# Three small unread tiles that shift the on-chip addresses of x's parts, the weights' parts and the small tiles

## The chip, the core and the metric

The kernel runs on one core of a Trainium2 chip, from one launch. The metric is the device time of that core in microseconds (us), as the median of repeated runs. All data lie in HBM at the start; the core has an on-chip memory of 128 partitions (SBUF), an accumulator memory (PSUM), and engines that run side by side: TensorE multiplies matrices, VectorE (DVE) and ScalarE (ACT) work element by element, GpSimd (POOL) does a little of both and issues some DMAs, and SyncE (SP) issues the others. A matmul on TensorE has two operands in SBUF: a stationary one of 128 x 128 elements, which is loaded first (a weight load, PEld in the profile), and a moving one of up to 512 columns, which is streamed through it.

## The reference, cut to what matters

The reference is a two-layer sequence encoder over 512 positions of 1024 channels in float32. Layer 0 mixes positions with a gated delta rule (8 heads, chunks of 64), layer 1 with gated linear attention (4 heads, chunks of 64). Each mixer is followed by a residual and a LayerNorm, then by a squared-ReLU MLP with 4096 hidden features, again with a residual and a LayerNorm.

```python
for i in range(DEPTH):                      # DEPTH = 2
    m = _mixer_gdn(x, ...) if i % 2 == 0 else _mixer_gla(x, ...)
    x = _layernorm(DEEPNORM_ALPHA * x + m, ln1_g[i], ln1_b[i])
    a = relu(matmul(x, mlp_w1[i]))          # 512 x 1024 by 1024 x 4096
    x = _layernorm(DEEPNORM_ALPHA * x + matmul(a * a, mlp_w2[i]), ln2_g[i], ln2_b[i])
```

Most of the arithmetic is in the large products: the input and output projections of the mixers and the two matrices of each MLP.

## The kernel before

**Products in three parts.** Every large float32 product is made of three matmuls. `split` (L85) turns a float32 tile into a high part (ACT, L96 or L106: the value rounded to the format fp32r) and a low part (DVE, L101: what the rounding left). `mm3` (L119 to L124) then issues high x high, high x low and low x high into the same PSUM bank. The weights are loaded by SP into `wst` tiles (L106, L115), and their parts go to `wh` and `wl`. The activations x stand transposed as `xth` and `xtl` (128 partitions, 8 blocks of 128 channels, 512 positions).

**Stages, in order.** `gdn` (to about 430 us): for each of 8 heads four projections of 128 columns (`pjk`, `pjq`, `pjv`, `pjz`: x moving, weights stationary, 512 columns), with the chunk work of other heads between them; then the output projection (`oa`, `ob`: weights moving). `mlp` of layer 0 (to about 740 us), `gla` (to about 990 us; `pjv` has x as the stationary operand and the weights moving), `mlp` of layer 1 (to the end).

**The MLP.** The first matrix of a group of features is multiplied with Strassen's scheme on 2 x 2 blocks (`Pair.products`, L475): seven products of 256 columns into the banks `fx` and `fyz`. Three of them read slices of `xth` and `xtl`; four read sums of such blocks, which `x_blocks` (L407) builds once per layer and splits into `xh3`, `xl3`, `xh5` ... `xl7` (printed by the profile as `xh` and `xl`). The stationary operand of all seven is a part of the weights in `wh` and `wl`. The second matrix (`second`, L548) goes the same way with 512 columns into `pX`, `pY`, `pZ`: the moving operand is `w2h` or `w2l`, the stationary one `ah` or `al`. In the main loop (L744) TensorE alternates: 12 matmuls of 256 columns (`fx`, `fyz`), then 6 of 512 columns (`pX`, `pY`, `pZ`), in an order written out by hand (`in_order`).

**Where tiles lie.** Each tile gets a fixed byte offset, the same in all 128 partitions, when the program is built. Pools stand one behind the other in the order in which `body` opens them (L1802): `const`, `big`, `wst`, `whl`, `small`, and behind these the pools of a stage. Inside a pool the tiles stand in the order of their first use; each is rounded up to 32 bytes. In the kernel before:

| tiles | pool | first offset | offset mod 128 |
|---|---|---|---|
| `ident`, five biases | const | 4224 | 0 (`ident`) |
| `xt0` to `xt3` (also `oh`), `xth`, `xtl` | big | 4896 | 32 |
| `wst` (3 buffers) | wst | 54048 | 32 |
| `wh`, `wl` (3 buffers each) | whl | 66336 | 32 |
| row statistics and the like | small | 90912 | 0 to 96 |
| constants for layer 1 (992 bytes, open from the first MLP to the end of `gla`) | gcst | 93984 | 32 |
| first MLP: `h`, `ah`, `al`, `w2r`, `w2h`, `w2l`, `xh`, `xl` | mlp | 94976 | 0 |
| second MLP: the same tiles, with no `gcst` ahead of them | mlp | 93984 | 32 |
| gla: `oth`, `otl`, `q`, `k`, `v` and others | gla | 94976 | 0 |
| gdn: `ol`, `sil`, `kt`, `qd` and others | gdn | 124800 | 0 |

All the large tiles are multiples of 128 bytes long, and the slices that the matmuls take (a block of 128 weight columns is 512 bytes, a block of 256 positions 1024 bytes) keep the offset of their tile mod 128.

Of the kernel before, what the change touches and what calls it, by code (L numbers as in the profile page):

```python
# [8 lines left out]
F32 = mybir.dt.float32  # L9
# [8 lines left out]
P = 128  # L18
# [10 lines left out]
class Ctx:  # L29


    def __init__(self, tc, nc, pools):
        self.tc, self.nc = tc, nc
        self.const, self.big, self.wst, self.whl, self.small = pools
        nc_ = nc
        self.ident = self.const.tile([P, P], F32, name="ident")
        make_identity(nc_, self.ident[:, :])

        self.bias = {}
        for i, v in enumerate((LN_EPS, RMS_EPS, -0.5 * math.log(P), 1.0 / D, -1.0 / D)):  # L40
            self.bias[v] = self.const.tile([P, 1], F32, name=f"bias{i}")
            nc.vector.memset(self.bias[v], v)
        self.xth = self.xtl = self.xt = None
        self.dma_i = 0
        nc.scalar.preload_act_table_set("natural_log_exp_and_others")

    def dma(self, out, in_):
# [1782 lines left out]
```

## Time and profile before

| | |
|---|---|
| median of 3 runs | 1331.79 us (1331.76 to 1331.99) |
| time of the profiled execution | 1330.95 us |
| its span, first to last instruction | 1329.0 us |
| mean granted TensorE clock | 0.997 |
| TensorE matmuls in the trace | 8659 |
| VectorE busy | 1108.9 us (83%) |
| ScalarE busy | 805.3 us (61%) |
| HBM read, written | 113.99 MB, 2.10 MB |

The profile comes from one execution. Its page gives busy times, 40 equal slices of the span, the chain of work that ended last, and groups of instructions by source line and tile. Matmuls overlap each other: the recorded length of one runs from its start to the (modelled) time its last result is out, so the sum of lengths says more than the engine can do, and what counts is the step from the start of one matmul to the start of the next. The timeline gives these starts. TensorE's line of the page covers the union of the recorded lengths.

### The profile page before, as it was taken

Reading aid. Unit: us, or ns where it says so; the run is one execution under the profiler, and the core shown is the slowest. Engines: PE = TensorE matmul, PEld = TensorE weight load, DVE = VectorE, ACT = ScalarE, POOL = GpSimd, SP = SyncE. Lnnn points to the kernel's source line nnn. Section 1 sums busy time; section 2 is a strip of 40 time slices with the busy share of each in tenths; the row PEclk is TensorE's granted clock in tenths of the full one; section 3 lists DMA queues with packets and bytes.
Section 4 is the critical chain, followed back from the end, with each engine's and each line's share of the span. In section 5 each row is a group of like instructions: output and inputs, shape, how many; then the busy total and the mean of one; then the engine's idle time right before and its main releaser. Section 6 shows DMA issues by size and latency. Waiting matters only on the chain.

```text
span 1329.0 us, 22303 instructions
## 1 busy us (share of the span) xinstructions
PE 1310.3 (99%) x8659; PEld 1120.2 (84%) x8659; DVE 1108.9 (83%) x1818; ACT 805.3 (61%) x1598; POOL 124.7 (9%) x177
## 2 busy tenths in 40 slices
PE   9999999999999999999999999999999999999996
PEld 7777877777877889999998888888889899999985
DVE  7787888878768988989988787867878789889888
ACT  4757666767643666566667754554466466566656
POOL 5000000000001810101101200000001001101011
PEclk9999999999999999999999999999999999999998
DMA  5210110111232574575548521211217365556465
GB/s 182 95 49 33 55 59 34 63 49 56 73 112 96 176 179 153 145 196 152 149 146 169 154 85 64 75 53 64 96 63 226 94 196 151 146 172 157 145 140 145
DMA packets 44044, 154.35 MB, mean 116 GB/s; under 512 B 5419, under 2 KB 5795, under 8 KB 43939
## 3 DMA queue, kind: packets, MB, share of 16 engines
q1 hardware_dynamic: 32163, 110.85, 24.6%
q0 software_dynamic: 11776, 42.08, 15.9%
q8 instruction: 68, 1.11, 0.3%
q14 instruction: 37, 0.30, 0.1%
HBM read 113.99 MB, written 2.10 MB: 87 GB/s over the span
## 4 chain that ended last, share of the span: by engine, by line
PE 92%; DVE 4%; ACT 3%; issue 1%; DVEq 0%; POOL 0%; ACTq 0%; POOLq 0%
PE fx L124 3%; PE fx L123 3%; PE fx L122 3%; PE pX L123 3%; PE pX L122 3%; PE pX L124 3%; PE pjv L122 3%; PE pjv L123 3%; PE pjv L124 3%; PE m L1692 3%; PE fyz L124 3%; PE fyz L122 3%; PE fyz L123 3%; PE pY L123 2%; PE pY L122 2%; PE pY L124 2%
## 5 line engine op out<-in xcount | busy, mean ns | idle before, releaser
L96 ACT CAST wh<-wst 128x1024 fp32r<-128x1024 f32 x152 | 159.5, 1049 | 115.9 <-PE fyz L123 38.2
L101 DVE TENSOR_TENSOR wl<-wst,wh 128x1024 fp32r<-128x1024 f32 x150 | 184.7, 1232 | 46.1 <-ACT wh L96 45.3
L101 DVE TENSOR_TENSOR w2l<-w2r,w2h 128x1024 fp32r<-128x1024 f32 x92 | 112.5, 1223 | 22.2 <-ACT w2h L96 22.2
L96 ACT CAST w2h<-w2r 128x1024 fp32r<-128x1024 f32 x94 | 98.4, 1048 | 45.1 <-PE pX L124 16.7
L400 POOL DMA_DIRECT2D w2r<-w2r x56 | 48.5, 896 | 497.4 <-DVE w2l L101 252.9
L96 ACT CAST ah<-h 128x1024 fp32r<-128x1024 f32 x56 | 58.9, 1051 | 40.4 <-PE pX L123 18.3
L448 DVE TENSOR_TENSOR wst<-wst 128x512 f32<-128x512 f32 x120 | 80.0, 688 | 0.4
L101 DVE TENSOR_TENSOR al<-h,ah 128x1024 fp32r<-128x1024 f32 x56 | 68.5, 1223 | 4.4 <-ACT ah L96 4.4
L123 PE MATMUL pX<-w2l,ah 128*128 128x512 f32 x168 | 66.2, 394 | 0.0
L122 PE MATMUL pX<-w2h,ah 128*128 128x512 f32 x168 | 66.1, 393 | 0.0
L124 PE MATMUL pX<-w2h,al 128*128 128x512 f32 x168 | 65.7, 391 | 0.0
L122 PE MATMUL pjv<-wh,xth 128*128 128x512 f32 x128 | 54.4, 425 | 0.0
L124 PE MATMUL fx<-xh,wl 128*128 128x256 f32 x192 | 54.3, 283 | 0.0
L124 PE MATMUL fyz<-xh,wl 128*128 128x256 f32 x192 | 54.2, 282 | 0.0
L122 PE MATMUL fx<-xth,wh 128*128 128x256 f32 x192 | 54.2, 282 | 0.0
L124 PE MATMUL fx<-xth,wl 128*128 128x256 f32 x192 | 54.2, 282 | 0.0
L123 PE MATMUL fx<-xtl,wh 128*128 128x256 f32 x192 | 54.2, 282 | 0.0
L122 PE MATMUL fyz<-xh,wh 128*128 128x256 f32 x192 | 54.2, 282 | 0.0
L123 PE MATMUL fx<-xl,wh 128*128 128x256 f32 x192 | 54.1, 282 | 0.0
L123 PE MATMUL fyz<-xl,wh 128*128 128x256 f32 x192 | 54.0, 281 | 0.0
L122 PE MATMUL fx<-xh,wh 128*128 128x256 f32 x192 | 53.8, 280 | 0.0
L123 PE MATMUL pj<-xtl,wh 128*128 128x256 f32 (+1 forms) x160 | 52.2, 328 | 0.2 <-DVE xtl L188 0.2
(536 smaller groups left out, 4326.2 us busy)
## 6 DMA issues: line engine op xcount, KB each, us to landing
wst<-in_w SPq DMA_DIRECT2D x68, 512.0 KB, 4.3
w2r<-in_w SPq DMA_DIRECT2D x60, 512.0 KB, 3.8
w2r<-w2r POOLq DMA_DIRECT2D x56, 512.0 KB, 5.3
wst<-in_a_in SPq DMA_DIRECT2D x32, 512.0 KB, 3.3
wst<-in_b_vr SPq DMA_DIRECT2D x16, 512.0 KB, 3.4
wst<-in_a_out SPq DMA_DIRECT2D x8, 512.0 KB, 3.3
wst<-in_b_in SPq DMA_DIRECT2D x8, 512.0 KB, 3.4
wst<-in_b_out SPq DMA_DIRECT2D x8, 512.0 KB, 3.3
```

Of the source, the lines that this page charges most:

```text
L96: h = nc.scalar.copy(hi, src)
L101: self.halves = h, nc.vector.tensor_tensor(lo, src, hi.bitcast(F32), ALU.subtract)
L122: mm(ps, ah, bh, start=start, stop=False, **kw)
L123: mm(ps, ah, bl, start=False, stop=False, **kw)
L124: self.last_mm = mm(ps, al, bh, start=False, stop=stop, **kw)
L400: nc.gpsimd.dma_start(blocks[a + (q,)], blocks[b + (q,)], accum_op=ALU.add)
L448: plus = lambda a, b: V.tensor_tensor(a, a, b, ALU.add)
L1692: T.matmul(ps[:, d, :], *ops(d), start=True, stop=True)
```

## The change

Three tiles are added that nothing reads: 96 bytes per partition at the end of `const`, 64 bytes at the head of `whl`, and 96 bytes at the head of `small`. Each is written once by a memset on VectorE.

```diff
         self.xth = self.xtl = self.xt = None
         self.dma_i = 0
+        for pool, n in ((self.const, 24), (self.whl, 16), (self.small, 24)):
+            nc.vector.memset(pool.tile([P, n], F32, name="room", bufs=1), 0.0)
         nc.scalar.preload_act_table_set("natural_log_exp_and_others")
```

The tiles behind them move. With the table above: `xt`, `xth`, `xtl` and `wst` move by 96 bytes, from 32 to 0 mod 128. `wh` and `wl` move by 160, from 32 to 64 mod 128. Everything behind `small`'s new tile moves by 256, so its offset mod 128 stays: the tiles of the first MLP, of `gla` and of `gdn` listed above stay at 0, those of the second MLP at 32. No instruction of the rest of the program is added, removed or reordered in the source.

## The prediction

> **What bounds the kernel now.** I read the page first, for the engine that sets the end.
>
> ```profile
> PE 1310.3 (99%) x8659; PEld 1120.2 (84%) x8659; DVE 1108.9 (83%) x1818; ACT 805.3 (61%) x1598; POOL 124.7 (9%) x177
> ...
> PE   9999999999999999999999999999999999999996
> ...
> PEclk9999999999999999999999999999999999999998
> ...
> PE 92%; DVE 4%; ACT 3%; issue 1%; DVEq 0%; POOL 0%; ACTq 0%; POOLq 0%
> ```
>
> TensorE is busy in every slice at full clock, and 92% of the chain that ended last is its own. DVE and ACT have slack. So a byte offset is worth what it does to the step from one matmul to the next. The timeline gives steps, and the layout table says which operands they join. Here are five runs of matmuls without a break, each by its first and a later start.
>
> ```profile
> 433.17 0.28 PE L122 MATMUL pj<-xth,wh 128*128 128x256 f32 x1
> ...
> 440.73 0.28 PE L122 MATMUL pj<-xth,wh 128*128 128x256 f32 x1
> ...
> 441.08 0.28 PE L122 MATMUL pj<-xth,ah 128*128 128x256 f32 x1
> ...
> 443.77 0.28 PE L124 MATMUL pj<-xth,al 128*128 128x256 f32 x1
> ...
> 500.95 0.28 PE L122 MATMUL fyz<-xh,wh 128*128 128x256 f32 x1
> ...
> 502.37 0.40 PE L122 MATMUL pX<-w2h,ah 128*128 128x512 f32 x1
> ...
> 704.64 0.40 PE L122 MATMUL pX<-wh,ah 128*128 128x512 f32 x1
> ...
> 707.44 0.40 PE L122 MATMUL pY<-w2h,ah 128*128 128x512 f32 x1
> ...
> 713.14 0.39 PE L123 MATMUL pZ<-w2l,ah 128*128 128x512 f32 x1
> ...
> 717.90 0.39 PE L123 MATMUL pZ<-xl,ah 128*128 128x512 f32 x1
> ```
>
> 256 columns, both operands at 32 mod 128: 63 steps in 7.56 us, 120 ns each. Moving at 32, stationary at 0: 23 steps in 2.69 us, 117 ns. Moving at 0, stationary at 32: 12 steps in 1.42 us, 118.3 ns. 512 columns, moving at 32, stationary at 0: 12 steps in 2.80 us, 233.3 ns. Both at 0: 21 steps in 4.76 us, 226.7 ns. So the offset of one operand against the other is seen: 32 bytes apart, short matmuls gain 2 to 3 ns and long ones lose 6 to 7. The common offset is not seen: long ones with both at 32 (`pj`, next fence) step at 226.
>
> In the lines view a matmul's recorded length is its step plus about 163 (283 against 120), so a group's mean tells its step.
>
> ```profile
> L124 PE MATMUL pjv<-wh,xtl 128*128 128x512 f32 x128 | 50.2, 392 | 0.0
> L123 PE MATMUL pjv<-wl,xth 128*128 128x512 f32 x128 | 50.0, 390 | 0.0
> ...
> L122 PE MATMUL pjq<-xth,wh 128*128 128x512 f32 x88 | 37.2, 423 | 0.0
> ...
> L122 PE MATMUL pj<-xth,wh 128*128 128x512 f32 x64 | 24.9, 389 | 0.0
> ```
>
> The projections step at 226 to 229 ns where nothing comes between; `pjq`'s 423 holds breaks for other work, which no offset removes.
>
> The two MLPs are a test inside this trace: same program, but in the first the block sums lie at 0 against weight parts at 32, in the second both at 32. The windows view over the same part of each:
>
> ```profile
> 467.00:697.00 230.00, 230.00 (x1484) 1.00 0.59 159
> ...
> 1044.00:1274.00 230.00, 230.00 (x1478) 1.00 0.57 153
> ```
>
> In 230 us the first gets through 6 matmuls more. At a mean of 230 / 1484 = 155 ns that is 0.9 us, for 576 `xh` matmuls. The lines view of the first window, then of the second:
>
> ```profile
> L123 PE MATMUL fx<-xl,wh 128*128 128x256 f32 x96 | 27.0, 281 | 0.0
> ...
> L124 PE MATMUL pX<-w2h,al 128*128 128x512 f32 x72 | 28.4, 394 | 0.0
> ```
>
> ```profile
> L123 PE MATMUL fx<-xl,wh 128*128 128x256 f32 x96 | 27.2, 283 | 0.0
> ...
> L124 PE MATMUL pX<-w2h,al 128*128 128x512 f32 x71 | 27.6, 389 | 0.0
> ```
>
> 32 apart, the short ones win 2 ns; the long one during which the next weights at 32 are loaded loses 5. The gain is mostly given back.
>
> **The change part by part.** *Memsets.* Three memsets of at most 128x24 on DVE, after the biases.
>
> ```profile
> 0.87 0.17 DVE L42 MEMSET bias<- 128x1 f32 x5 [0.87 <-PEq L1819]
> ...
> 1.12 2.65 DVE L1141 MEMSET pz<- 128x512 uint32 x5
> ...
> 4.61 1.05 ACT L1226 CAST xth<-xt 128x1024 fp32r<-128x1024 f32 x1 [2.53 <-DMA xt<-in_xt]
> 5.69 1.40 DVE L1227 TENSOR_TENSOR xtl<-xt,xth 128x1024 fp32r<-128x1024 f32 x1 [1.89 <-ACT xth L1226]
> ```
>
> Five bias memsets take 0.17 us, so three take 0.1 to 0.2. They push the `pz` memsets back, and DVE then idles 1.89 us ahead of `xtl`: cost nothing; without that cover 0.2 us. No queue of POOL, SP or ACT is touched, and no wait is added.
>
> *`xt` and `wst` from 32 to 0, `wl` and `wh` to 64, for DVE, ACT and the DMAs.* DVE's and ACT's same work at 0 (first window) and at 32 (second):
>
> ```profile
> L101 DVE TENSOR_TENSOR w2l<-w2r,w2h 128x1024 fp32r<-128x1024 f32 x40 | 48.8, 1221 | 8.2 <-ACT w2h L96 8.2
> L96 ACT CAST w2h<-w2r 128x1024 fp32r<-128x1024 f32 x40 | 42.0, 1049 | 17.9 <-PE pX L124 8.4 <-PE pZ L124 7.9 <-DMA w2r<-w2r 1.0
> ```
>
> ```profile
> L101 DVE TENSOR_TENSOR w2l<-w2r,w2h 128x1024 fp32r<-128x1024 f32 x40 | 48.8, 1221 | 12.0 <-ACT w2h L96 12.0
> L96 ACT CAST w2h<-w2r 128x1024 fp32r<-128x1024 f32 x40 | 41.9, 1047 | 21.6 <-PE pX L124 8.4 <-PE pZ L124 7.9 <-DMA w2r<-w2r 4.9
> ```
>
> 1221 and 1221, 1049 and 1047 ns: nothing, with or without cover. A DMA's landing could change only the first, exposed one (ACT waits 2.53 us for it): I bound it by 0.2 us either way and take 0.
>
> *x's parts against weight parts, 0 apart to 64 apart.* This is the bulk: about 1,700 matmuls of 512 columns (`pjq`, `pjk`, `pjz` and gdn's `pjv` 296 x 3, gla's `pjv` 128 x 3, `pj` 64 x 3, `oa` 80 x 3), and about 1,280 of 256 (`fx` and `fyz` from `xth`, `xtl` 288 x 3, the rest `pj`, `pjq`, `pjk`). No two operands of an fp32r matmul in this trace lie 64 apart, so I bound the price by the extremes of rows that are there (the tile view's min, median, max; the first `oa` is gdn's, the second gla's).
>
> ```profile
> L122 PE MATMUL oa<-wh,oh x48: 388/397/504, 334.8 to 397.4; 128*128 128x512 f32 x48
> ...
> L123 PE MATMUL oa<-wl,oth x32: 389/396/398, 936.4 to 966.8; 128*128 128x512 f32 x32
> ...
> L122 PE MATMUL fx<-xh,wh x96: 277/279/285, 472.7 to 693.1; 128*128 128x256 f32 x96
> ```
>
> Less 163: a long one steps at 225 to 235, a short one at 114 to 122, whatever its neighbours. Against 228 and 120 today: -3 to +7 ns for the long, -6 to +2 for the short; together from -12.8 to +14.5 us. I take 0. Reason: what differs between the rows is whether two operands that advance in strides are in step, and the difference at 32 is small and of opposite sign for short and long. If it repeats every 64 bytes, 64 apart is 0 apart again. That nothing depends on the common offset fits an effect of neighbouring pieces of a row, not of large blocks. It is a choice, the weakest of this sum.
>
> *Block sums against weight parts.* First MLP: 32 apart to 64. Second MLP: its block sums stay at 32, and the weights go to 64, so 0 apart to 32. With 64 as 0, the MLPs change places: +0.9 and -0.9 us. At the steps themselves: 576 x 1.7 ns = 1.0 us each, before the long ones give back their part.
>
> *Output projection of gla* (`oa`, 96 long ones): 32 apart (step 396 - 163 = 233) to 64. With 64 as 0: 96 x -5 ns = -0.5 us. gdn's `ol` third of 48: within 0.2 us.
>
> Sum: 1330.95 - 0.5 = 1330.45 us on the profiled execution's scale, whose span is 1329.0 with 1.95 us around it. The median lies 0.84 us above that execution: 1331.3.
>
> A rule speaks against any effect. The Trainium skill, page "TensorE: Matmul & The Clock Gate", section "Step-by-step: what each phase is for", says the streamed operand and the weight load have read ports of their own: "Loading the next tile's weights doesn't steal SBUF read bandwidth from the running matmul." By it no offset would matter and the sum would be 1330.95. The trace disagrees, with 233.3 against 226.7 ns, so I give the rule no chance of its own. The same page, section "Back-to-back issue gap", puts a warm matmul at N / 2.4 + 2.5 ns: 216 and 109 ns for these widths, under every step seen here. By that floor, as an estimate, the faster case below would reach about 1294 us; no run here shows an fp32r step that short.
>
> **The rivals.** *64 apart parts the two reads (faster).* If the effect repeats every 128 bytes, 64 may be the best place. For it: steps of 225 and 114 occur, and the excess over the columns' own time is there to be won. Against it: they are single minima between longer ones, never a lasting rhythm. Price: 1,700 x -3 - 1,280 x 6 - 576 x 4.3 (first MLP) - 0.9 (second MLP) = -16 us: 1330.95 - 16 + 0.84 = 1315.7.
>
> *Part of that (faster).* The short ones take the 117 ns of the 32-apart rows and the long ones keep their rhythm: 1,280 x -3 = -3.8, second MLP -0.9: 1327.1.
>
> *64 acts as 32 does (slower).* Place: every projection with 512 columns. Their rhythm of 226 to 229 ns becomes the 233.3 of `pX<-wh,ah`: +5.3 x 1,700 = +9.0; short ones 1,280 x -3 = -3.8; second MLP -0.9. Sum +4.3: 1331.79 + 4.3 = 1336.1. It decides when the long ones lose over 3.2 ns each. For it: the only offset besides 0 in this trace does just that. Against: many long matmuls of gdn are cut into short runs by other work (the 423 of `pjq`) and never settle into the rhythm, which trims the 9.0. At the long ones' worst (235) with no gain on the short it would be +12.
>
> *The change misses part of its target.* The block sums of the second MLP are not brought to 0, since `gcst` is closed there. That is in the sum; it makes the two MLPs cancel.
>
> **How the numbers follow.** 0.2%, or 2.7 us, is about what a measurement of this kernel tells from no change. No difference (1329 to 1333): 0.50. Faster: 0.31, of it full parting (about 1316) 0.15 and partial (1327 and between) 0.16. Slower: 0.19, about 1336. The range of 1315 to 1338 takes in all of these and leaves out only the far ends of both. Likeliest: 1331.3; its own range 1329 to 1333.
>
> **What would show it.** Right: projections in unbroken runs still at 389 to 392 (512 columns), `fx` from `xth` at 283; in the first MLP `fx<-xl,wh` up to 283 and `pX<-w2h,al` down to 389, in the second 281 and 394; DVE's and ACT's means unchanged. Wrong: `pj<-xth,wh` of 512 columns at 385 or 396, or `fx<-xth,wh` under 280: then 64 apart is a place of its own, and all matmuls of the bulk go with it. Memsets that delay `xtl` would show as the first `pjk` starting later than now.

## The result, and the profile after

The changed kernel takes 1329.2 us (median of 16 runs, 1328.33 to 1329.99), the kernel before in the same comparison 1331.6 us (16 runs, 1330.6 to 1332.25). The ratio is 0.9983, 95% interval 0.9976 to 0.9991: 2.4 us less, or 0.17%. The span of the profiled execution went from 1329.0 to 1326.3 us.

The total is close to the forecast, but the interval leaves out 1: the change does make a difference, and the steps are not those forecast. First the page of the changed kernel: busy time of each engine.

```profile
PE 1307.9 (99%) x8659; PEld 1115.2 (84%) x8659; DVE 1107.6 (84%) x1821; ACT 804.9 (61%) x1598; POOL 125.6 (9%) x177
```

The same 8,659 matmuls, in the same order, with TensorE as full as before; VectorE has three instructions more, the memsets. So the difference again lies in the steps between matmuls. The timeline of the changed kernel (start, recorded length, line, operands), a first and a later start of each of four unbroken runs:

```profile
432.94 0.28 PE L124 MATMUL pj<-xth,wh 128*128 128x256 f32 x1
...
440.76 0.28 PE L124 MATMUL pj<-xth,wh 128*128 128x256 f32 x1
...
443.94 0.39 PE L124 MATMUL pj<-xth,wh 128*128 128x512 f32 x1
...
452.34 0.40 PE L124 MATMUL pj<-xth,wh 128*128 128x512 f32 x1
...
504.02 0.28 PE L124 MATMUL fx<-xth,wh 128*128 128x256 f32 x1
...
505.43 0.39 PE L124 MATMUL pX<-w2h,ah 128*128 128x512 f32 x1
...
1099.06 0.28 PE L124 MATMUL fx<-xth,wh 128*128 128x256 f32 x1
...
1100.43 0.39 PE L124 MATMUL pY<-w2h,ah 128*128 128x512 f32 x1
```

In all four, x's parts are moving and the weights for the next matmul lie 64 bytes further mod 128 ("64 ahead" from here on); only the last step of the two runs of twelve goes over to the second matrix. The first run makes 69 steps in 7.82 us, 113.3 ns each, where the same run stepped at 120 before. The second makes 36 steps in 8.40 us, 233.3 ns each; these were 226.7. The last two are twelve short matmuls each, in the main loop of the first and of the second MLP: 1.41 us (117.5 ns a step) and 1.37 us (114.2). So short matmuls gain and long ones lose, and short ones at one and the same distance have two rhythms.

The lines view of the changed kernel shows what that means for whole groups (count, then busy us and mean ns):

```profile
L126 PE MATMUL pjv<-wh,xtl 128*128 128x512 f32 x128 | 50.4, 394 | 0.0
L125 PE MATMUL pjv<-wl,xth 128*128 128x512 f32 x128 | 50.1, 391 | 0.0
L124 PE MATMUL pjq<-xth,wh 128*128 128x512 f32 x88 | 37.4, 425 | 0.0
...
L124 PE MATMUL pj<-xth,wh 128*128 128x512 f32 x64 | 25.3, 395 | 0.0
```

The unbroken `pj` lost 6 ns a matmul (389 before), but `pjq`, cut up by other work, only 2 (423), and gla's `pjv` 1 or 2 (392 and 390). The lines view inside the two windows of the MLPs, first MLP and then second:

```profile
L126 PE MATMUL pX<-w2h,al 128*128 128x512 f32 x73 | 28.4, 389 | 0.0
...
L125 PE MATMUL fx<-xtl,wh 128*128 128x256 f32 x96 | 27.0, 281 | 0.0
...
L125 PE MATMUL fx<-xl,wh 128*128 128x256 f32 x96 | 26.8, 279 | 0.0
```

```profile
L126 PE MATMUL pX<-w2h,al 128*128 128x512 f32 x71 | 28.0, 394 | 0.0
...
L125 PE MATMUL fx<-xl,wh 128*128 128x256 f32 x96 | 26.9, 280 | 0.0
...
L125 PE MATMUL fx<-xtl,wh 128*128 128x256 f32 x93 | 25.7, 276 | 0.0
```

The first MLP's long matmuls are at 389 now (394 before); the second MLP's short ones from `xtl` are at 276. The lines view of the kernel before has 283 for these, in the same window:

```profile
L123 PE MATMUL fx<-xtl,wh 128*128 128x256 f32 x94 | 26.6, 283 | 0.0
```

A window fixed in time holds slightly other work once a stage begins earlier, so for the time of a stage I take the same matmul in both traces, by its place in TensorE's order: numbers 3,649 and 5,132 (near the ends of the first MLP's main loop) and 6,988 and 8,464 (the second's). The timeline of the kernel before, then of the changed one:

```profile
467.07 0.28 PE L122 MATMUL fx<-xth,wh 128*128 128x256 f32 x1
...
697.01 0.28 PE L122 MATMUL fx<-xth,wh 128*128 128x256 f32 x1
...
1044.05 0.28 PE L122 MATMUL fx<-xth,wh 128*128 128x256 f32 x1
...
1274.00 0.28 PE L124 MATMUL fx<-xth,wl 128*128 128x256 f32 x1
```

```profile
467.72 0.28 PE L124 MATMUL fx<-xth,wh 128*128 128x256 f32 x1
...
695.12 0.28 PE L124 MATMUL fx<-xth,wh 128*128 128x256 f32 x1
...
1043.20 0.28 PE L124 MATMUL fx<-xth,wh 128*128 128x256 f32 x1
...
1271.24 0.28 PE L126 MATMUL fx<-xth,wl 128*128 128x256 f32 x1
```

The first loop went from 229.94 to 227.40 us, the second from 229.95 to 228.04. Done for the whole trace, and each step sorted by the operands that it joins, this gives the account of the 2.7 us between the two profiled executions (us, after less before):

| where | difference |
|---|---|
| long projections x by weights in gdn, from 20 us on (739) | +0.84 |
| the same in gla (`pjv` 384, others 144) | +1.04 |
| `pj` of 512 columns (95 in each MLP) | +1.21 |
| short ones from x's parts to weights: second MLP (537), first (469) | -2.99, -0.96 |
| short ones from block sums to weights: second (531, counted with 84 from x's parts to `ah` and `al`), first (531) | +0.32, -0.16 |
| short ones from block sums to `ah` (45 each) | -0.55 |
| long ones of the second matrix: first MLP (571 inside, 81 ahead of `wh`) | -1.29, -0.49 |
| the same, second MLP (595 and 82) | -0.27, +0.64 |
| all the rest (parts between -0.3 and +0.3 that cancel) | 0.0 |

So a gross gain of 6.7 us stands against a loss of 4.0 (the negative and the positive rows). Two of the gains are of matmuls whose own distance did not change: the 45 + 45 from block sums to `ah`, and the 571 of the second matrix (`w2h`, `w2l` against `ah`, `al`: 0 apart before and after).

### The profile page after: what moved, and what is told of

It reads as the page before. It is cut to its first block, busy times and chain, and to the rows that moved or that the text cites. A ratio compares the mean times of both kernels' runs of the same rounds, so it can differ in the third digit from the quotient of the medians.

```text
span 1326.3 us, 22306 instructions
## 1 busy us (share of the span) xinstructions
PE 1307.9 (99%) x8659; PEld 1115.2 (84%) x8659; DVE 1107.6 (84%) x1821; ACT 804.9 (61%) x1598; POOL 125.6 (9%) x177
## 4 chain that ended last, share of the span: by engine, by line
PE 64%; DVE 3%; ACT 1%; issue 0%; DVEq 0%; POOL 0%; POOLq 0%; ACTq 0%
PE fx L124 3%; PE fx L126 3%; PE fx L125 3%; PE pX L125 3%; PE pX L124 3%; PE pX L126 3%; PE fyz L124 3%; PE fyz L126 3%; PE fyz L125 3%; PE pjv L126 2%; PE pjv L124 2%; PE pY L125 2%; PE pjv L125 2%; PE pY L124 2%; PE pY L126 2%; PE scp L990 2%
## 5 line engine op out<-in xcount | busy, mean ns | idle before, releaser
L103 DVE TENSOR_TENSOR w2l<-w2r,w2h 128x1024 fp32r<-128x1024 f32 x92 | 112.3, 1221 | 22.2 <-ACT w2h L98 22.0
```

Source lines behind the costliest of these rows:

```text
L103: self.halves = h, nc.vector.tensor_tensor(lo, src, hi.bitcast(F32), ALU.subtract)
```

## The experiments

**Theories.** A: a matmul's step follows from the distance between its moving operand and the next stationary one, mod 128, each distance with its own pair of steps (short, long). B: what counts is where x's parts lie by themselves, at a multiple of 128. D, formed after the first four runs: the distance allows several rhythms, and what a run of matmuls is entered from decides which one it takes. N and H, and any other letter, are explained in the expectation that uses them. Each version is compared with the kernel before, run on the same chip: 1331.20 us for the first four versions (21 runs), 1331.21 for the next four (22), 1330.97 for the last two (14).

**w_at_0**: x's parts at 0 as in the change, the weights at 0 too.

```diff
-        for pool, n in ((self.const, 24), (self.whl, 16), (self.small, 24)):
+        for pool, n in ((self.const, 24), (self.small, 40)):
```

> x's parts at 0 mod 128 as in the change, the weights' parts back to 0 apart from them (whl without its unread tile; everything behind small where the change has it). Theory A (the step follows the offset between the moving operand and the weights that are loaded meanwhile): unbroken runs of pj go back to 120 ns (256 columns) and 226.7 (512 columns), gla's pjv mean back to 390 to 392; time about 1331. Theory B (x's parts on a multiple of 128 are what counts): pj of 256 columns stays at 113, time stays near 1329.

1330.69 us, ratio 0.9997 (0.9988 to 1.0005). Its timeline, x's parts and weights 0 apart again:

```profile
433.37 0.28 PE L124 MATMUL pj<-xth,wh 128*128 128x256 f32 x1
...
440.57 0.28 PE L124 MATMUL pj<-xth,wh 128*128 128x256 f32 x1
```

60 steps in 7.20 us: 120 ns, as before the change. B falls: x's place by itself changes no step. The MLPs went apart (first +1.52 us, second -2.01), since their block sums now stand 0 and 32 from the weights instead of 32 and 0; that is the exchange of places that the prediction had meant, at about twice its 0.9.

**x_stays**: the same distance of 64 made without moving x (x at 32, weights at 96).

```diff
-        for pool, n in ((self.const, 24), (self.whl, 16), (self.small, 24)):
+        for pool, n in ((self.whl, 16), (self.small, 48)):
```

> x's parts and wst stay at 32 mod 128 as before the change; the weights' parts go to 96, so they are 64 apart from x, and 64 apart from the block sums of the second MLP (96 from those of the first). Theory A: pj of 256 columns steps at 113 and of 512 columns at 233, as with the change; fx from xh in the second MLP falls from 120 to about 113 to 115, worth 2 to 4 us against the change: time 1325 to 1328. Theory B: x is not on a multiple of 128, so pj steps at 120 and the time is that of before, 1331.6.

1331.02 us, ratio 1.0 (0.9991 to 1.0009). `pj` steps at 113.3 and 233.4 ns as in the change, so the distance counts and not the place. But the gain that A expected with it did not come. The lines view of this version in the second MLP's window:

```profile
L125 PE MATMUL fx<-xtl,wh 128*128 128x256 f32 x93 | 26.1, 281 | 0.0
```

281, not 276, at the same distance of x from the weights. A misses something; the rows of the change already hinted at it, with 281 in one MLP and 276 in the other.

**w_at_96** and **w_at_128**: distances of 96 and 128.

```diff
-        for pool, n in ((self.const, 24), (self.whl, 16), (self.small, 24)):
+        for pool, n in ((self.const, 24), (self.whl, 24), (self.small, 16)):    # w_at_96
+        for pool, n in ((self.const, 24), (self.whl, 32), (self.small, 8)):     # w_at_128
```

> x's parts at 0, the weights' parts at 96 mod 128 (32 below the next multiple). Theory A with a period of 128: a step of its own, near the 32-apart rows of before: pj of 256 columns at 116 to 118, of 512 columns at 231 to 234. Theory C (the period is 64, offsets other than a multiple of 64 are alike): the same as 32 apart, 117 and 233, but then 64 apart would have stayed at 120, which the change's trace already speaks against.

> x's parts at 0, the weights' parts 128 bytes further than a multiple they would share with x. Theory A with a period of 128: the same steps as w_at_0, 120 ns and 226.7 ns. A longer period (256 or more): steps unlike those, for pj of 256 columns 113 to 118.

One run each: 1331.37 and 1332.4 us, within the spread of the kernel before (1330.26 to 1332.44), so these two are read by their steps alone. At 96, short ones step at 117.4 and long ones at 234.2. At 128 I had expected the steps of 0 apart. The timeline of w_at_128:

```profile
433.26 0.28 PE L124 MATMUL pj<-xth,wh 128*128 128x256 f32 x1
...
440.38 0.28 PE L124 MATMUL pj<-xth,wh 128*128 128x256 f32 x1
...
443.94 0.40 PE L124 MATMUL pj<-xth,wh 128*128 128x512 f32 x1
...
446.73 0.39 PE L124 MATMUL pj<-xth,wh 128*128 128x512 f32 x1
```

60 steps in 7.12 us, 118.7 ns, and 12 steps in 2.79 us, 232.5 ns: not 120 and 226.7. Miss: the effect does not repeat every 128 bytes either. From here on I count distances mod 512, the length of a slice of weights; that is a choice, and no run shows that 512 is the period.

**x_by_stage**: the change, but x's parts 64 bytes further in both mixers, so that they are 0 apart from the weights where long matmuls prevail, and 64 apart in the MLPs.

```diff
-    def new_x(self):
-        self.xth = self.big.tile([P, KT, S], F32R, name="xth", tag="xth")
-        self.xtl = self.big.tile([P, KT, S], F32R, name="xtl", tag="xtl")
+    def new_x(self, lag=0):
+        self.xth, self.xtl = [
+            self.big.tile([P, KT * S + 128], F32R, name=n, tag=n)[:, lag:lag + KT * S].rearrange("p (k s) -> p k s", s=S)
+            for n in ("xth", "xtl")]
...
-                c.new_x()
+                c.new_x(16)
...
-        c.new_x()
+        c.new_x(16)
```

> The change, with x's parts moved by 64 bytes in the two mixers alone: there x and the weights' parts are 0 apart, in the MLPs the weights stay 64 ahead of x. Theory A (what the change lost are the long matmuls of the projections, 233 for 227 ns, since their weights moved 64 ahead of x): gdn's and gla's projections return to their old steps, worth 1.6 + 1.0 us, the short ones of the MLPs keep theirs: 1326 to 1327. Theory D (the step is set by the rhythm that a run happens to enter, and offsets only reshuffle it): the projections return, but the MLPs change too, by up to 2 us either way: 1325 to 1330.

1327.21 us, ratio 0.9969 (0.9957 to 0.9981). It was not run side by side with the change, but all its six runs (1326.66 to 1327.59) lie below the change's fastest (1328.33). Its lines view:

```profile
L124 PE MATMUL pjq<-xth,wh 128*128 128x512 f32 x88 | 37.1, 422 | 0.0
```

`pjq` is back at 422. Same matmul against same matmul, gdn's long projections differ by +0.02 us from the kernel before and gla's by +0.07 (the change: +0.84 and +1.04), and the main loops keep -2.48 and -1.95. So the loss in the mixers was the price of 64 ahead for the long ones, and it can be had back alone.

**sums_64**: the change, with the pools of both MLPs placed so that the weights are 64 ahead of the block sums too. **both**: this and x_by_stage together.

```diff
-        for pool, n in ((self.const, 24), (self.whl, 16), (self.small, 24)):
+        for pool, n in ((self.const, 24), (self.whl, 16), (self.small, 120)):
...
+        if out is not None:
+            V.memset(pool.tile([P, 120], F32, name="room", bufs=1), 0.0)
```

> The change, with the pools of both MLPs moved so that the weights' parts are 64 ahead of the block sums also (mod 512), as they are of x. Theory A: all fx and fyz step at 113 (in the change 118 to 120 in the rows from xh), worth 2 to 7 us: 1322 to 1327. Theory D: the runs may fall into the rhythm of 117.7 ns instead: 1327 to 1330, and nothing is won where they do.

> x_by_stage and sums_64 together. Theory A: both gains add up: 1319 to 1325. Theory D: the gain of the projections is there, that of the MLPs depends on the rhythm: 1324 to 1328.

1330.61 us, ratio 0.9996 (0.9988 to 1.0005), and 1329.39, ratio 0.9983 (0.9974 to 0.9992). By A, with its 113 ns, some 1,150 block-sum matmuls more should have won several us; both came out slower than the versions without the edit (1329.2 and 1327.21). The lines view of sums_64, second MLP:

```profile
L125 PE MATMUL fx<-xl,wh 128*128 128x256 f32 x96 | 27.0, 281 | 0.0
...
L125 PE MATMUL fx<-xtl,wh 128*128 128x256 f32 x94 | 26.4, 281 | 0.0
```

All short ones of the MLPs went into the rhythm of 117.7, also those from x's parts that had been at 276: an edit to the block sums changed the step of matmuls that it does not touch. A falls as the whole story, D stands. In size D was off for `both` by 1.4 us (it said 1324 to 1328); in the profiled execution, 0.74 us against the kernel before is a later start, in the first 20 us.

A trace that was there already says the same. In the second MLP of x_stays the weights stand 64 ahead of x's parts, as in sums_64, and 320 ahead of the block sums, where sums_64 has 64. The tiles lie at other places, and all 21 group means of the loop are the same to within 1 ns: 281 for `fx` from `xtl` and `xl`, 395 for `pX<-w2l,ah`, 389 for `pX<-w2h,al`. So for the block sums 64 and 320 act alike, which hints at a period of 256 and does not prove it.

**w_64_behind**: the change, with the weights 448 bytes ahead of x mod 512, that is 64 behind.

```diff
-        for pool, n in ((self.const, 24), (self.whl, 16), (self.small, 24)):
+        for pool, n in ((self.const, 24), (self.whl, 112), (self.small, 56)):
```

> x's parts at 0, the weights' parts 64 bytes behind a multiple of 512 above x (448 ahead) instead of 64 ahead. In the runs so far operands that lie so step at 226 to 229 (long) and 117.8 (short). Theory A with a sign (ahead and behind differ): gdn's projections stay near their steps of before, short ones from x at 117.8, time within 1328 to 1332. If only the distance counted: 233 and 113, as with the change.

One run: 1330.14 us. In gdn the long projections cost 0.24 us more than before the change (64 ahead: 0.84), while gla's `pjv`, whose moving operand is the weights, so that x is now 64 ahead of it, went the other way. The lines view of this version:

```profile
L125 PE MATMUL pjv<-wl,xth 128*128 128x512 f32 x128 | 50.5, 394 | 0.0
```

394 against 390 before and 391 in the change. So ahead and behind differ for the mixers' long matmuls. Not everywhere, though: `pj` of the first MLP steps at 233.3 ns here as well. So the sign holds in part, on one run.

**first_as_second** and **second_as_first**, the test of D: on top of x_by_stage, all distances mod 512 between the operands of the first MLP are made those of the second (weights 96 behind the block sums, not 64), or those of the second made those of the first. x's parts stay 64 from the weights in both.

```diff
+        if out is None:                                                       # first_as_second
+            V.memset(pool.tile([P, 8], F32, name="room", bufs=1), 0.0)
```

```diff
+        if out is not None:                                                   # second_as_first
+            V.memset(pool.tile([P, 120], F32, name="room", bufs=1), 0.0)
```

> The version with x's parts placed by stage, and 32 bytes of room ahead of the first MLP's tiles: every distance between operands in the first MLP is then, mod 512, the one that the second MLP has in the changed kernel (weights 96 behind the block sums instead of 64 behind; x's parts against the weights 64 ahead as before). Theory N (the distances of the neighbouring matmuls decide in which rhythm a run of twelve short ones goes on): fx from xth and xtl in the first MLP leave the rhythm of 117.7 ns for that of 113.3, group means of 277 in place of 281, the step from weights to weights goes from 228 to 236, the windows 467 to 697 and 1044 to 1274 have equal counts within 2, and the time is 1327 to 1328.5 (the first MLP then gains about 2.0 us against the kernel before instead of 2.5). Theory H (the rhythm belongs to the stage: other traffic, other engines, or the time at which the stage begins): the first MLP stays at 281 and its gain shrinks by more than 1 us, 1328.5 to 1330.

> The version with x's parts placed by stage, and 480 bytes of room ahead of the second MLP's tiles: every distance between operands in the second MLP is then, mod 512, the one that the first MLP has in the changed kernel (weights 64 behind the block sums instead of 96 behind). Theory N (the distances of the neighbouring matmuls decide): fx from xth and xtl in the second MLP go from means of 277 to 281, pX, pY and pZ from 394 to 389 or 390, the step from sums to sums falls from 120.8 to 118.0, and the second window ends with the count of the first; the time is 1326.3 to 1327.2. Theory H (the rhythm belongs to the stage): fx from xth stays at 277 while pX, pY and pZ settle at 389, which would give 1325 to 1326.

first_as_second: 1329.16 us, ratio 0.9985 (0.9976 to 0.9995). second_as_first: 1326.03 us, ratio 0.9963 (0.9949 to 0.9977), the best of all versions. The lines view of first_as_second in the first MLP, then of second_as_first in the second:

```profile
L126 PE MATMUL pX<-w2h,al 128*128 128x512 f32 x73 | 28.7, 394 | 0.0
...
L125 PE MATMUL fx<-xtl,wh 128*128 128x256 f32 x95 | 26.2, 276 | 0.0
```

```profile
L126 PE MATMUL pX<-w2h,al 128*128 128x512 f32 x71 | 27.6, 389 | 0.0
...
L125 PE MATMUL fx<-xtl,wh 128*128 128x256 f32 x92 | 25.9, 281 | 0.0
```

276 and 394 have moved to the first MLP, 281 and 389 to the second: each MLP took the means of the other, to the nanosecond, with the distances. N is right about the rows, and H (the rhythm belongs to the stage) falls. The rows repeat from trace to trace: with the weights 64 behind the sums, `fx<-xtl,wh` is at 281 in four loops (the first MLP of the change, of x_by_stage and of second_as_first, and the second MLP of second_as_first), and with 96 behind at 276 in four (the second MLP of the change, of x_by_stage and of first_as_second, and the first MLP of first_as_second). The edits also move the MLP's tiles themselves, but their places alone do not decide: in x_stays they lie mod 512 where the change has them, and the second MLP's row is at 281, not 276.

The times of the loops go the same way. The timeline of second_as_first, matmuls 6,988 and 8,464:

```profile
1042.51 0.28 PE L124 MATMUL fx<-xth,wh 128*128 128x256 f32 x1
...
1269.13 0.28 PE L126 MATMUL fx<-xth,wl 128*128 128x256 f32 x1
```

226.62 us against 228.04 in the change and 229.95 before. In first_as_second the first loop took 228.83 us against 227.40 in the change. My expectation of 1327 to 1328.5 for it forgot that the first loop does seven matmuls more than the second in the same time before the change: made like the second it should win about 1 us less than I wrote, 7 times 155 ns, and it did (1.12 us against the kernel before, not 2.0). By the total alone neither run would have decided: 1329.16 lies in the range written down for H (1328.5 to 1330), and 1326.03 lies between those of H (1325 to 1326) and N (1326.3 to 1327.2). N missed both totals; the rows and the loops decide. The fixed windows count 1489 and 1490 matmuls in first_as_second, as N said, but 1497 and 1491 in second_as_first, where the second window runs 4.9 us past the loop.

That also names the better arrangement. The 276 of the short ones comes with 394 for the long ones, and the whole loop is better with 281 and 389: a short rhythm of 113 ns is not the aim in itself.

## Why the prediction was right, and where it was not

**The total** (1331.3, own range 1329 to 1333): measured 1329.2, at its lower edge. Small, as forecast, but as the difference of 6.7 us won and 4.0 lost, not because little happens. That the two nearly cancel is luck: nothing in the prediction says that they would.

**Memsets at nothing**: right. The start of the changed kernel in the timeline:

```profile
1.02 0.14 DVE L46 MEMSET room<- 128x24 f32 x3
1.22 2.65 DVE L1143 MEMSET pz<- 128x512 uint32 x5
...
5.52 1.22 DVE L1229 TENSOR_TENSOR xtl<-xt,xth 128x1024 fp32r<-128x1024 f32 x1 [1.64 <-ACT xth L1228]
...
7.97 0.71 PE L1252 MATMUL pjk<-xth,wh 128*128 128x512 f32 x2
```

Three memsets in 0.14 us push `pz` back by 0.10, and DVE still idles 1.64 us ahead of `xtl`. The first `pjk` starts at 7.97 us (8.28 before); over all versions it starts between 7.47 and 9.00 us, so 0.2 us more or less could not be seen here.

**Nothing for DVE, ACT and DMAs**: right. In the first MLP's window of the changed kernel:

```profile
L103 DVE TENSOR_TENSOR w2l<-w2r,w2h 128x1024 fp32r<-128x1024 f32 x40 | 48.7, 1218 | 8.3 <-ACT w2h L98 8.2
...
L98 ACT CAST w2h<-w2r 128x1024 fp32r<-128x1024 f32 x40 | 41.8, 1045 | 18.0 <-PE pX L126 7.9 <-PE pZ L126 7.5 <-DMA w2r<-w2r 2.4
```

1218 and 1045 ns, against 1221 and 1049.

**x's parts 64 apart from the weights, taken at 0**: this is the step that failed, and with it the words "If it repeats every 64 bytes, 64 apart is 0 apart again". The prediction's own sign of it came: `pj` of 512 columns at 395, `fx` from x's parts at 276 to 279 in the second MLP. 64 apart is a place of its own; at 128 apart, too, the steps are not those of 0. The prediction had bounded the long ones by -3 to +7 ns and the short by -6 to +2, and the truth lay at both ends at once: long ones in a steady run +6.6, short ones -2 to -7, a little beyond the bound. Taking the middle of a range as the value hid two large terms of opposite sign.

**Block sums, +0.9 and -0.9**: the direct part is small and has the opposite sign (-0.16 first, +0.32 second, of which the block sums alone make +0.21). What the loops did (-2.54, -1.91) came from x's short ones and from long ones whose distance never changed. The prediction priced each matmul by its own pair of operands; the exchange of the two MLPs shows that the neighbours' pairs are part of the price. Of the four MLP rows named as the sign of being right, three came within 1 ns (`pX<-w2h,al` at 389 in the first and 394 in the second, `fx<-xl,wh` at 280 in the second), while the first MLP's `fx<-xl,wh` went to 279, not up to 283. The reason given for all four, that 64 acts as 0, was wrong, so rows that fit are no proof of a reason.

**gla's `oa`, -0.5 us**: did not come. The tile view of the changed kernel:

```profile
L125 PE MATMUL oa<-wl,oth x32: 391/394/398, 935.5 to 965.9; 128*128 128x512 f32 x32
```

Median 394 against 396; all 96 of them together differ by 0.01 us. 32 and 64 apart are the same for these.

**The rivals.** "64 acts as 32 does" was right about its mechanism for the long ones (233.3 ns) and wrong in size: 5.3 ns for 1,700 matmuls was to cost 9.0 us, and gdn, gla and `pj` together paid 3.1. (By its own terms a loss of 2.8 ns on each long one, not 3.2, would have evened out its gains of 3.8 and 0.9 us.) It had itself named the reason for the smaller size: the 513 long projections of gdn that no other work breaks up averaged 230.8 ns before, not 228, and went to 233.3, only 2.5 more. "Part of that" was right that the short ones gain and wrong that the long ones keep their rhythm. "Full parting" needed long ones at 225; none were. The Trainium skill's rule quoted in the prediction, by which no offset would matter (page "TensorE: Matmul & The Clock Gate", section "Step-by-step: what each phase is for"), would give one time for the change and all ten versions; the medians of those with five runs or more lie between 1326.03 and 1331.02 us.

## What to carry to other kernels

When matmuls follow each other without a break, the byte distance between what is streamed and what is loaded next can be worth some ns a step, with opposite signs for different widths: choose it stage by stage, as x_by_stage does, and judge it by the whole loop, as second_as_first shows. When a range for an unknown cost is wide and two kinds of instruction lie at its two ends, a value in the middle is no forecast; price the kinds apart. And two stages of one program that do the same work at different places are a free experiment: exchange their places, and see whether the rows move along.

## What the runs showed of the hardware

Mean steps in unbroken runs, by how far the next stationary operand lies ahead of the moving one (mod 512), from the starts in the traces:

| distance | short (256 columns), ns | long (512 columns), ns |
|---|---|---|
| 0 | 120 | 226.7 (226 to 236 in the main loop) |
| 32 | 118.3 (runs of twelve) | 232.7 (no run: 80 single steps ahead of short ones, 227 to 235) |
| 64 | 113.3 or 117.7 | 233.3 |
| 96 | 117.4 | 234.2 |
| 128 | 118.7 | 232.5 |
| 448 (64 behind) | 117.7 | 229 to 233.3 |
| 480 (32 behind) | 117 | 233.3 |

I had not expected that the most regular of these rhythms are multiples of one unit: 113.3, 120, 226.7 and 233.3 are 17, 18, 34 and 35 times 6.67 ns, and three steps of the 117.7 rhythm are 53 times that. The other values of the table, such as 117.4, 118.3, 232.5 and 234.2, are means and no such multiples. In the second MLP of the kernel before, where the step varies between 226 and 236, the start of a matmul modulo 6.67 ns accounts for some 65% of the variance of 766 long steps, and for some 85% of that of the 477 inside the main loop (fits on the trace that they were made from). It would fit D, if a run that begins at another point of the unit goes on in another rhythm; no run tested this. What the unit is, and why a distance of 64 gives short ones 113.3 in one surrounding and 117.7 in another, stays open: in the main loops the surrounding distances select it, but the runs do not show how.

Distances do not always settle it. The `pj` run ahead of the first MLP steps at 113.3 ns in the change and at 117.8 in x_by_stage. In second_as_first every tile lies as in x_by_stage up to there, since its edit comes with the second MLP, and the run is at 113.3 again. The timeline of x_by_stage, then of second_as_first, 69 steps each:

```profile
432.67 0.28 PE L124 MATMUL pj<-xth,wh 128*128 128x256 f32 x1
...
440.80 0.28 PE L124 MATMUL pj<-xth,wh 128*128 128x256 f32 x1
```

```profile
432.84 0.28 PE L124 MATMUL pj<-xth,wh 128*128 128x256 f32 x1
...
440.66 0.28 PE L124 MATMUL pj<-xth,wh 128*128 128x256 f32 x1
```

8.13 us against 7.82: two executions with the same places take two rhythms, as D says of what a run is entered from. The main loops showed no such change between traces. Not tried was a search over these surroundings.
